# Routing with the first weights' splits behind the gathers and low parts on GpSimd; last sums, squares, statistics and output by quarters ahead of the general path

## Chip, core and metric

One Trainium2 chip, one core of it. The metric is device time in microseconds (us) of one execution; it is given as the median of several runs. Engines are called as in the profile: PE (TensorE; PEld is its weight load), DVE (VectorE), ACT (ScalarE), POOL (GpSimd), SP (SyncE, which issues most transfers). PE's clock has two levels, 1.2 and 2.4 GHz; the profile gives the granted clock as a share of the upper one.

## What is computed

A trunk of two pre-norm residual layers over 256 tokens of width 1024. Each has a mixer (a convolution branch and a bidirectional state-space branch); the first has a dense SwiGLU after it, the second eight SwiGLU experts of which each token takes two. A final RMSNorm gives the output. The change touches only the second layer's expert part and the final norm:

```python
def top2_moe(h, router_w, router_b, w_gate, w_up, w_down):
    t = h.reshape(bsz * seq_len, d)
    logits = (t @ router_w + router_b).astype(jnp.float32)
    top_val, top_idx = lax.top_k(logits, TOP_K)
    top_w = jax.nn.softmax(top_val, axis=-1)
    gates = jnp.sum(one_hot(top_idx, 8) * top_w[..., None], axis=1)
    for e in range(8):
        out = out + gates[:, e:e+1] * swiglu(t, w_gate[e], w_up[e], w_down[e])
...
x = x + top2_moe(rms_norm(x, g), ...)
return rms_norm(x, final_norm_g)
```

## The kernel before

Activations lie transposed: `x` is 8 tiles of 128 channels by 256 tokens. Precision comes from splitting a float32 operand into a rounded high part and a low part (`fp32r`), so a product of two split operands is three matmuls.

**Order.** Each engine runs its instructions in the order in which the Python code was executed: `ordered()` chains PE, DVE and ACT, and for the experts SP too. An instruction that waits therefore holds up everything behind it on its engine.

**Routing** (`route`, a generator, L1189). The router's logits come from `route_feed`, with the mean square of each token. `rms_of` turns it into `rs` (`rms_s`, 12 small DVE instructions). Then DVE makes `lg` (logits), the two largest, and `asg` (who goes where); PE counts tokens per expert (`rank`); DVE turns the ranks into one-hot matrices `oh`. Meanwhile `turn` transposes the normed activations on PE (tile `misc` in PSUM, two buffers), ACT rounds them to `hth`, and DVE takes the rest as `htl`. After the first one-hot, `alone` gathers expert 0's tokens: eight groups of four matmuls `misc<-oh,hth` and `misc<-oh,htl`, each copied out by ACT. The rest of the generator orders the experts by load (`ei`), gives each its ranks (`srank`) and gates (`gr`), and writes 14 further one-hots. `gate_rs(0)` multiplies `gr` by `oh`, and DVE copies the result (`gs`).

**Weights** (`moe_stream`). SP loads 1 MB at a time into 8 buffers `raw`. For the five fullest experts (j < NL) each half of a load is split by ACT into `wh` and by DVE into `wl` (L93, L75 through `split`); a pair is called a unit here. There are four buffers each of `wh` and `wl`. `get()` first fills a queue up to three units ahead, then takes one. `get.prime()` only fills. Before routing starts, `moe` calls `get.prime()`, so three units are split ahead of the routing.

**Experts** (`moe`). `first(v)` multiplies gate and up weights (four units, six matmuls each), `second(v)` the down weights (two units) into `py`. After an expert's last block, `back` scales `py` by the gate (ACT `yh`, DVE `yl`), `oht(j)` transposes the one-hot (PE, then a copy by ACT), and PE multiplies the two back into token order, in four quarters that `into` adds to `x`. The three emptiest experts do the same unsplit (`back_few`, `ys`).

**End.** `rest` is a general path for an expert with more than 128 tokens; it is skipped by a branch on `cnt` on every engine. Behind it `final` takes squares of `x` (ACT, `sq`), sums them on PE with 16 one-column products (32 passes in the trace), makes the scale (12 DVE instructions, two transposes, an ACT copy), scales `x` in eight pieces `o` and stores four quarters from SP.

Of the kernel before, what the change touches and what calls it, by code (L numbers as in the profile page):

```python
# [19 lines left out]
T = 256  # L20
# [8 lines left out]
NB = DFF // 256  # L29
# [29 lines left out]
class Body:  # L59
# [1129 lines left out]
    def route(self):  # L1189
        nc = self.nc  # L1190
        sp = self.rp
        hth = self.slot("hth", [128, 2, D], F32R)
        htl = self.slot("htl", [128, 2, D], F32R)
        self.hth, self.htl = hth, htl

        def turn(k4, b):

            ps = self.misc()
            for k in range(4):
                self.tr(ps[:, k * 128:(k + 1) * 128], self.xg[k4][:, k, b * 128:(b + 1) * 128])  # L1200
            s = slice(512 * k4, 512 * k4 + 512)
            nc.scalar.activation(hth[:, b, s], ps, AF.Copy)

            def low():
                self.sub(htl[:, b, s], ps, hth[:, b, s].bitcast(F32))
            return low

        pl = self.acc()
        for b in range(2):
            nc.tensor.transpose(pl[:, b * 8:b * 8 + 8], self.lt[:, b * 128:(b + 1) * 128], self.ident[0:8, 0:8])  # L1210
        lows = [turn(0, b) for b in range(2)]
        rs = self.rs

        gr = sp.tile([128, 2, NE, 2], F32, name="gr0")
# [32 lines left out]
        self.sub(d[:, :, 0], mx[:, :, 0], mx[:, :, 1])  # L1247
        self.sub(d[:, :, 1], mx[:, :, 1], mx[:, :, 0])
        nc.scalar.activation(d, d, AF.Tanh, scale=0.5)
        for f in lows:  # L1250
            f()
        lows = [turn(1, b) for b in range(2)]

        rank = sp.tile([128, 2, NE], F32, name="rank")
        self.stt(rank, ps[:, 0:16].rearrange("p (b e) -> p b e", b=2), 1.0, asg, ALU.add, ALU.mult)
# [2 lines left out]
        self.oh = oh  # L1258
        for b in range(2):
            nc.vector.tensor_scalar(oh[:, b, 0], self.iota, rank[:, b, 0:1], None, op0=ALU.is_equal)  # L1260
        for f in lows:
            f()
        yield
        nc.vector.tensor_scalar(d, d, 0.5, 0.5, op0=ALU.mult, op1=ALU.add)
        nc.vector.tensor_copy(gr[:, :, :, 1], two(rs))
# [66 lines left out]
    def moe_stream(self, items, ahead):  # L1332

        items, ready = deque(items), deque()
        first = [True]

        def prep():
            j, w, at, split = items.popleft()
            raw = self.raw8()
            src = self.a[w][(self.expert_of(j),) + at].rearrange("o p f -> p (o f)")  # L1340
            ins = self.nc.sync.dma_start(raw, src)
            if first[0]:
                self.behind(ins.ins, self.last_raw.ins)
                first[0] = False
            if split:
                for h in range(2):
                    yield self.split(raw[:, 1024 * h:1024 * h + 1024], 1024)
            else:
                yield raw

        now = [iter(())]

        def prime():
            while len(ready) <= ahead:
                u = next(now[0], None)
                if u is None:
                    if not items:
                        return
                    now[0] = prep()
                    u = next(now[0])  # L1360
                ready.append(u)

        def get():
            prime()
            return ready.popleft()
        get.prime = prime
        return get

    def moe(self):
# [18 lines left out]
                j, b = seq[t - 1]  # L1388
                items.append((j, "m_down", (b,), j < NL))
        get = self.moe_stream(items, 2)  # L1390
        get.prime()
        route = self.route()
        next(route)
        oh = self.oh
# [53 lines left out]
                tok[e + i] = [lambda k, h=h, i=i: tiles[h](k)[:, i] for h in range(2)]  # L1448

        def gather1():  # L1450
            x = [self.slot("x1", [128, 8, 2, 128], F32R) for _ in range(2)]
# [57 lines left out]
            self.sub(al, pv, ah.bitcast(F32))  # L1509
            return ah, al  # L1510

        py, pys = {}, {}
        extra = deque()

        def second(v, a):
            j, b = v
            last = b == NB - 1
            if j >= NL:
                if b == 0:
                    pys[j] = self.psx.tile([128, 512], F32, name="pys")  # L1520
                w = get()
                for k in range(2):
                    for h in range(2):
                        self.mm(pys[j][64 * h:64 * h + 64], a[:, 64 * k:64 * k + 64],
                                w[:, 1024 * k + 512 * h:1024 * k + 512 * h + 512], b == 0 and k == 0, last and k == 1)
                if last:
                    extra.append(back_few(j, pys.pop(j)))
                    next(extra[-1])
                return
            if b == 0:  # L1530
                py[j] = self.psx.tile([128, D], F32, name="py")
            ah, al = a
# [20 lines left out]
        def into(i, ps):  # L1553
            xq = self.x[:, 2 * i:2 * i + 2]
            self.add(xq, xq, ps.rearrange("p (f t) -> p f t", f=2))
            self.sums[i] += 1
            if self.sums[i] == NE:
                self.last_sum(i)

        def back(j, py):  # L1560
# [6 lines left out]
            o = oht(j, F32R)  # L1567
            yield
            for i in range(4):
                ps = self.misc()  # L1570
# [8 lines left out]
        def back_few(j, py):  # L1579
            y = self.ep.tile([128, 512], F32, name="ys")  # L1580
            nc.scalar.activation(y, py, AF.Copy, scale=gss[j][:, 0:1])
            o = oht(j, F32)
            yield
            for i in range(4):
                ps = self.misc()
# [17 lines left out]
                gate_rs(j)  # L1603
            yield

        self.sums = [0] * 4
        alone()
        for _ in route:
            pass
        gate_rs(0)  # L1610
        side = deque([small(), rates(range(NL, NE)), gather1(), rates(range(1, NL))])
        sl = None
# [23 lines left out]
                    side.popleft()  # L1636
        while extra:
            more()

    def rest(self):  # L1640

# [2 lines left out]
        with tc.If(n > self.cap):  # L1644
            hf = [t.bitcast(F32) for t in (self.hth, self.htl)]
            with tc.For_i(0, NE, 1) as e:
# [49 lines left out]
                for d in range(8):  # L1696
                    ps = self.misc()
                    self.mm(ps[:, :T], y[:, d * 128:(d + 1) * 128], oht, True, True)
                    self.add(self.x[:, d], self.x[:, d], ps[:, :T])

    def moe_consts(self):
        nc, cp = self.nc, self.cp
# [9 lines left out]

    def last_sum(self, i):

        pass

    def final(self):
        nc = self.nc
        rs, rb = self.rms_stat()
        g = self.col("gfin")  # L1720
        dst = self.out.rearrange("(k p) t -> p k t", p=128)
        o = self.slot("o", [128, 8, T])
        for k in range(8):
            self.stt(o[:, k], self.x[:, k], g[:, k:k + 1], rb, ALU.mult, ALU.mult)
            if k % 2:
                nc.sync.dma_start(dst[:, k - 1:k + 1], o[:, k - 1:k + 1])

    def specs(self):

# [66 lines left out]
    def run(self):  # L1796
        pool = self.pool
        with ExitStack() as ctx:
# [44 lines left out]
            with ExitStack() as c2:  # L1843
                self.sp = pool(c2, "slotf", 1)
                self.final()


_NAMES = ("xt", "par", "cdg", "bc", "bd", "w_in", "w_cproj", "w_glu", "w_sproj", "w_out", "f_gate", "f_up",
# [87 lines left out]
```

## Time and profile before

| | |
|---|---|
| runs | 1428.27 us median of 3 (1427.89 to 1429.31) |
| profiled execution | 1430.8 us, span 1429.0 us, mean granted clock 0.972 |
| busy | PE 1341.0 us (94%), PEld 1079.3 (76%), DVE 952.3 (67%), ACT 686.1 (48%), POOL 84.3 (6%) |
| routing, from the last products with `x` to the first expert product | 663.0 to 681.9 us |
| experts | 681.9 to 1409.0 us |
| final norm and output | 1409.0 to 1429.0 us |

The span runs from the first to the last instruction of one core. A busy PE is not PE at its peak. An idle stretch of an engine costs time only if the engine is the one the end waits for; in the expert stage that is PE, while in routing and in the final norm one engine after the other is waited for.

### The profile page before, as it was taken

The numbers are of one execution on the slowest core, as the hardware profiler recorded it, in microseconds if no ns is written. First come the engines' busy times: TensorE is split into PE (matmuls) and PEld (weight loads), VectorE is DVE, ScalarE is ACT, GpSimd is POOL, SyncE is SP. The second block draws the span as 40 slices with busy tenths as digits, with TensorE's granted clock in tenths as the row PEclk, the third lists the DMA queues.
The fourth block names the chain that finished last, engine by engine and source line by source line (L and its number), as shares of the span: only waits on it lengthen the run. The fifth ranks groups of instructions, "written<-read, shape, count | busy, mean of one in ns | idle before, by whom it ended". The sixth has DMA issues, their size and how long they took to land. (4 is left out here: it accounts for less than half of the span.)

```text
span 1429.0 us, 23540 instructions
## 1 busy us (share of the span) xinstructions
PE 1341.0 (94%) x9291; PEld 1079.3 (76%) x9291; DVE 952.3 (67%) x1413; ACT 686.1 (48%) x968; POOL 84.3 (6%) x148
## 2 busy tenths in 40 slices
PE   6989989999998969888999999999999999999995
PEld 5868879999998858886876666667676676666663
DVE  7696675788885465765775665667666666666663
ACT  3432344454444524443675555555555555555551
POOL 1052220000120040000000000000000000000000
PEclk9999999999999989998999999999999999999996
DMA  5284444566678394564689999998999999999970
GB/s 218 97 258 150 168 133 150 191 220 207 221 234 285 132 299 130 180 222 159 236 313 362 394 347 407 405 417 338 405 421 419 365 418 351 414 368 416 409 301 31
DMA packets 78307, 399.73 MB, mean 280 GB/s; under 512 B 13024, under 2 KB 15728, under 8 KB 44400
## 3 DMA queue, kind: packets, MB, share of 16 engines
q1 hardware_dynamic: 65504, 371.22, 68.0%
q0 software_dynamic: 8448, 26.31, 5.7%
q8 instruction: 75, 1.23, 0.4%
q10 hardware_dynamic: 4240, 0.64, 0.3%
q14 instruction: 40, 0.33, 0.1%
HBM read 386.51 MB, written 11.62 MB: 279 GB/s over the span
## 5 line engine op out<-in xcount | busy, mean ns | idle before, releaser
L75 DVE TENSOR_TENSOR wl<-raw,wh 128x1024 fp32r<-128x1024 f32 x460 | 549.5, 1222 | 220.5 <-ACT wh L93 220.2
L93 ACT ACTIVATE wh<-raw 128x1024 fp32r<-128x1024 f32 x460 | 470.5, 1054 | 77.1 <-issue 35.8
L116 PE MATMUL acc<-wh,x 128*128 128x512 f32 x880 | 293.9, 401 | 0.0
L116 PEld LDWEIGHTS acc<-wh,x 128*128 128x128 f32 x880 | 165.5, 188 | 44.9 <-ACT wh L93 8.9
L116 PE MATMUL acc<-wl,x 128*128 128x512 f32 x440 | 173.0, 393 | 0.0
L116 PE MATMUL acc<-hf,wh 128*128 128x256 f32 x704 | 128.4, 285 | 0.0
L116 PE MATMUL acc<-raw,xs 128*64 128x256 f32 x1056 | 127.9, 384 | 0.0
L116 PE MATMUL acc<-hh,wh 128*128 128x256 f32 x352 | 105.1, 298 | 7.0 <-ACT hh L636 3.1
L116 PE MATMUL acc<-xg,raw 128*128 128x256 f32 x448 | 103.2, 388 | 6.8 <-DMA raw<-in_w_in 6.8
L116 PEld LDWEIGHTS acc<-hf,wh 128*128 128x128 f32 x704 | 109.0, 190 | 0.2
L116 PEld LDWEIGHTS acc<-raw,xs 128*64 128x64 f32 x1056 | 71.2, 137 | 46.9 <-issue 17.5
L116 PE MATMUL acc<-hh,wl 128*128 128x256 f32 x352 | 103.0, 293 | 1.7 <-DVE wl L75 1.7
L116 PE MATMUL acc<-hl,wh 128*128 128x256 f32 x352 | 102.9, 292 | 0.0
L116 PE MATMUL acc<-hf,wl 128*128 128x256 f32 x352 | 99.9, 284 | 2.0 <-DVE wl L75 2.0
L116 PEld LDWEIGHTS acc<-xg,raw 128*128 128x128 f32 x448 | 85.8, 195 | 19.1 <-ACT xg L682 6.8
L116 PEld LDWEIGHTS acc<-wl,x 128*128 128x128 f32 x440 | 83.1, 189 | 18.0 <-DVE wl L75 1.7
L116 PE MATMUL py<-wh,mah 128*128 128x512 f32 x220 | 89.6, 407 | 0.0
L116 PE MATMUL py<-wh,mal 128*128 128x512 f32 x220 | 86.1, 391 | 0.0
L116 PE MATMUL py<-wl,mah 128*128 128x512 f32 x220 | 86.0, 391 | 0.0
L1508 ACT ACTIVATE mah<-misc 128x256 fp32r<-128x256 f32 x55 | 21.1, 384 | 128.6 <-PE misc L124 128.3
L116 PEld LDWEIGHTS acc<-hh,wh 128*128 128x128 f32 x352 | 70.7, 201 | 10.8 <-issue 4.0
L75 DVE TENSOR_TENSOR mal<-misc,mah 128x256 fp32r<-128x256 f32 x55 | 23.3, 423 | 74.9 <-ACT mah L1508 74.8
(290 smaller groups left out, 2002.6 us busy)
## 6 DMA issues: line engine op xcount, KB each, us to landing
raw<-in_m_gu SPq DMA_DIRECT2D x176, 1024.0 KB, 8.0
raw<-in_m_down SPq DMA_DIRECT2D x88, 1024.0 KB, 8.3
raw<-in_w_in SPq DMA_DIRECT2D x56, 512.0 KB, 4.1
raw<-in_f_gate SPq DMA_DIRECT2D x22, 512.0 KB, 3.5
raw<-in_f_up SPq DMA_DIRECT2D x22, 512.0 KB, 3.7
raw<-in_f_down SPq DMA_DIRECT2D x22, 512.0 KB, 3.5
raw<-in_w_out SPq DMA_DIRECT2D x16, 512.0 KB, 3.5
hs<-hc POOLq DMA_DIRECT2D x32, 142.0 KB, 5.4
```

The lines of the kernel that those rows point to most:

```text
L75: return self.nc.vector.tensor_tensor(out, a, b, op=op)
L93: self.nc.scalar.activation(h, raw, AF.Copy)
L116: return self.nc.tensor.matmul(out, l, r, start=start, stop=stop, **kw)
L1508: nc.scalar.activation(ah, pv, AF.Copy)
```

## The change

Five edits.

1. `moe` no longer calls `get.prime()` ahead of routing. Instead the loop that drains the routing generator calls `get.one()` at each of its steps, which splits one unit if fewer than three are ready. This loop stands behind `alone`.
2. All four `turn`s stand together ahead of the ranks. ACT copies `misc` a second time, to SBUF (`full`), and POOL subtracts `htl = full - hth`; DVE did this from PSUM.
3. `oht(j)` is made one block earlier, ahead of the products of block NB-2.
4. `last_sum`, called when a quarter of `x` has its last sum, takes that quarter's squares and the product of `x` with the final norm's weights (`o`, ACT). The quarter's products with `ones` are queued, and issued on PE behind the next quarter's add.
5. `finish` makes the scale and multiplies the four quarters of `o` by it straight from PSUM, and stores them from SP and ACT in turn. It stands ahead of the branch on `cnt`. The general path ends in its own `final`. For this the slots `x1` are taken first.

```diff
@@ route
+        self.x1 = [self.slot("x1", [128, 8, 2, 128], F32R) for _ in range(2)]
...
+            full = self.c2("full", [128, 512])
             nc.scalar.activation(hth[:, b, s], ps, AF.Copy)
-            def low():
-                self.sub(htl[:, b, s], ps, hth[:, b, s].bitcast(F32))
-            return low
+            nc.scalar.copy(full, ps)
+            nc.gpsimd.tensor_tensor(htl[:, b, s], full, hth[:, b, s].bitcast(F32), op=ALU.subtract)
...
-        lows = [turn(0, b) for b in range(2)]
+        for k4 in range(2):
+            for b in range(2):
+                turn(k4, b)
@@ moe_stream
+        def one():
+            n = len(ready)
+            if n <= ahead:
+                prime(n)
@@ moe
-        get.prime()
         route = self.route()
...
@@ second
+                if b == NB - 2:
+                    ohts[j] = oht(j, F32)
...
             if self.sums[i] == NE:
+                while self.queued:
+                    self.queued.pop(0)()
                 self.last_sum(i)
...
         alone()
         for _ in route:
-            pass
+            get.one()
...
         while extra:
             more()
+        self.finish()
@@ last_sum
+        sq = self.c2("sq", [128, 2, T])
+        nc.scalar.activation(sq, self.x[:, 2 * i:2 * i + 2], AF.Square)
+        for k in (2 * i, 2 * i + 1):
+            nc.scalar.activation(self.o[:, k], self.x[:, k], AF.Copy, scale=g[:, k:k + 1])
+        def products():
+            for d in range(2):
+                for b in range(2):
+                    self.mm(self.fin[:, b:b + 1], sq[:, d, b * 128:(b + 1) * 128], self.ones, ...)
+        self.queued.append(products)
@@ finish
+        rs = self.rms_of(self.fin[:, :2])
+        ps = self.acc()
+        for b in range(2):
+            self.tr(ps[:, b * 128:(b + 1) * 128], rs[:, b:b + 1].to_broadcast([128, 128]))
+        for i in range(4):
+            oq = self.o[:, 2 * i:2 * i + 2]
+            self.mul(oq, oq, ps[:, None, :T].to_broadcast([128, 2, T]))
+            (nc.sync, nc.scalar)[i % 2].dma_start(dst[:, 2 * i:2 * i + 2], oq)
```

On ACT, from the rounding of the gates' difference (`dd`) to the splits, before (`x_7275` and `x_7276` are expert 0's gathered high and low parts):

```order
L1249 ACTIVATE dd<-dd 128x4
L1202 ACTIVATE hth<-misc 128x512 x2
L1431 CAST x_7275<-misc 128x256
L1431 CAST x_7276<-misc 128x256
L1431 CAST x_7275<-misc 128x256
L1431 CAST x_7276<-misc 128x256
L1431 CAST x_7275<-misc 128x256
L1431 CAST x_7276<-misc 128x256
L1431 CAST x_7275<-misc 128x256
L1431 CAST x_7276<-misc 128x256
L93 ACTIVATE wh<-raw 128x1024 x4
```

The same place on ACT in the change (the gathered parts are `x_7269` and `x_7270`):

```order
L1205 COPY full<-misc 128x512
L1251 ACTIVATE dd<-dd 128x4
L1432 CAST x_7269<-misc 128x256
L1432 CAST x_7270<-misc 128x256
L1432 CAST x_7269<-misc 128x256
L1432 CAST x_7270<-misc 128x256
L1432 CAST x_7269<-misc 128x256
L1432 CAST x_7270<-misc 128x256
L1432 CAST x_7269<-misc 128x256
L1432 CAST x_7270<-misc 128x256
L93 ACTIVATE wh<-raw 128x1024 x7
```

The three `wh` that stood ahead of the first `hth` now stand behind the last of the eight copies.

On DVE, from the second rank sum to the one-hots, before:

```order
L1290 TENSOR_REDUCE srank<-t 128x8
L75 TENSOR_TENSOR t<-pm,gr 128x64
L1294 TENSOR_REDUCE gr<-t 128x8
L75 TENSOR_TENSOR t<-pm,gr 128x64
L1294 TENSOR_REDUCE gr<-t 128x8
L1295 COPY gr<-rms_s 128x16
L1301 TENSOR_SCALAR oh<-iota,srank 128x128 x14
```

In the change (here `t_7343` and `gr_7234` are single buffers of `t` and `gr`):

```order
L1287 TENSOR_REDUCE srank<-t_7343 128x8
L75 TENSOR_TENSOR wl<-raw,wh 128x1024
L75 TENSOR_TENSOR t_7343<-pm,gr_7234 128x64
L1291 TENSOR_REDUCE gr<-t_7343 128x8
L75 TENSOR_TENSOR t_7343<-pm,gr_7234 128x64
L1291 TENSOR_REDUCE gr<-t_7343 128x8
L1292 COPY gr<-rms_s 128x16
L75 TENSOR_TENSOR wl<-raw,wh 128x1024
L1298 TENSOR_SCALAR oh<-iota,srank 128x128 x14
```

A further `wl` stands between `ei` and `pm`, the first of the rank sums. The three `wl` stood ahead of `lg` before.

On PE, the end of the experts, before (`oht_13145` is the last small expert's transposed one-hot):

```order
L116 MATMUL misc<-oht_13118,yh 128x256
L116 MATMUL misc<-oht_13118,yl 128x256
L116 MATMUL misc<-oht_13145,ys 128x256 x8
L1643 TENSOR_LOAD cnt
L1644 COMPARE_AND_BRANCH
```

In the change (`oht_13072` is that one-hot, `acc` the sums of squares):

```order
L116 MATMUL misc<-oht_13072,ys 128x256 x4
L116 MATMUL acc<-ones,sq 128x1 x4
L116 MATMUL misc<-oht_13072,ys 128x256 x2
L116 MATMUL acc<-ones,sq 128x1 x4
L116 MATMUL misc<-oht_13072,ys 128x256 x2
L116 MATMUL acc<-ones,sq 128x1 x8
L124 MATMUL acc<-ident,rms_s 128x128 x2
L1651 TENSOR_LOAD cnt
L1652 COMPARE_AND_BRANCH
```

The sums of squares moved from behind the branch to between the last experts' products, and the two transposes of the scale with them.

## Rows read from the trace of the kernel before

**Rows 1.** Busy time, granted clock and transfers by stage (window, length, engines, PEclk, DMA share, GB/s).

```profile
665.40:675.40 10.00, 4.12 (x19) 3.72 (x19) 7.89 (x25) 2.23 (x5) 0.00 (x0) 0.51 0.32 119
681.90:1394.40 712.50, 704.63 (x3668) 498.50 (x3669) 460.90 (x518) 396.75 (x539) 0.57 (x1) 1.00 0.94 376
```

**Rows 2.** Timeline of routing (start, length in us, instruction, idle before and its releaser).

```profile
665.36 3.50 DVE L75 TENSOR_TENSOR wl<-raw,wh 128x1024 fp32r<-128x1024 f32 x3
668.77 0.17 DVE L75 TENSOR_TENSOR lg<-acc,rms_s 128x16 f32<-128x16 f32 x1
673.06 0.17 DVE L87 SCALAR_TENSOR_TENSOR rank<-acc,asg 128x16 f32<-128x16 f32 x1 [1.06 <-PE acc L116]
674.64 0.69 DVE L75 TENSOR_TENSOR htl<-misc,hth 128x512 fp32r<-128x512 f32 x1 [0.67 <-ACT hth L1202]
675.38 0.93 PEld L116 LDWEIGHTS misc<-oh,hth 128*128 128x128 f32 x4 [0.96 <-DVE htl L75]
677.76 0.22 DVE L75 TENSOR_TENSOR pm<-iota,sf 128x64 f32<-128x64 f32 x1
680.03 2.83 DVE L1301 TENSOR_SCALAR oh<-iota,srank 128x128 fp32r<-128x128 f32 x14
681.41 0.59 PE L116 MATMUL misc<-gr,oh 128*128 128x2 f32 x4
681.87 0.49 PE L116 MATMUL acc<-wh,x 128*128 128x512 f32 x1
681.88 1.06 ACT L93 ACTIVATE wh<-raw 128x1024 fp32r<-128x1024 f32 x1
683.86 1.20 DVE L75 TENSOR_TENSOR wl<-raw,wh 128x1024 fp32r<-128x1024 f32 x1
687.50 0.51 PE L116 MATMUL misc<-oh,hth 128*128 128x384 f32 x2
```

**Rows 3.** Two us behind the last sum (columns as in Rows 1).

```profile
1409.00:1411.00 2.00, 0.00 (x0) 0.00 (x0) 0.00 (x0) 1.67 (x3) 0.00 (x0) 0.68 0.00 0
```

**Rows 4.** PE's waits from 683 to 1405 us (us in total, times, longest).

```profile
PE misc L116 <- ACT oht L1550: 6.5, 7, 1.2
PE misc L116 <- DVE yl L87: 2.7, 4, 0.7
```

**Rows 5.** All engines' waits from 800 to 1390 us, the weight loads of second products.

```profile
PEld py L116 <- ACT wh L93: 11.1, 29, 0.4
```

**Rows 6.** The GpSimd group of the largest mean, before 640 us.

```profile
L347 POOL COPY tabo<-pw 64x256 f32<-64x256 f32 x6 | 6.9, 1156 | 0.3
```

**Rows 7.** Timeline of the last expert and the final norm.

```profile
1397.07 0.39 PE L116 MATMUL misc<-oht,yl 128*128 128x256 f32 x1 [0.67 <-DVE yl L87]
...
1404.36 3.90 PE L116 MATMUL misc<-oht,ys 64*128 64x256 f32 x16
1408.30 0.69 DVE L75 TENSOR_TENSOR x<-x,misc 128x512 f32<-128x512 f32 x1 [0.18 <-PE misc L116]
1409.22 1.67 ACT L219 ACTIVATE sq<-x 128x512 f32<-128x512 f32 x3 [5.65 <-DVEq L1644]
1411.69 6.95 PE L116 MATMUL misc<-ones,sq 128*128 128x1 f32 x32 [3.43 <-PEq L1644]
1418.68 0.16 DVE L225 TENSOR_SCALAR rms_v<-misc 128x2 f32<-128x2 f32 x1 [9.69 <-PE misc L116]
1421.06 0.69 PE L124 MATMUL misc<-ident,rms_s 128*128 128x128 f32 x2 [2.42 <-DVE rms_s L87]
1422.19 3.25 DVE L87 SCALAR_TENSOR_TENSOR o<-x,par,rstdb 128x256 f32<-128x256 f32 x8 [1.19 <-ACT rstdb L145]
1423.10 2.75 SPq L1726 DMA_DIRECT2D out_t<-o  x4
```

**Rows 8.** SP's waits from 683 to 1400 us, at the branch.

```profile
SPq L1644 <- SPq L1644: 7.4, 2, 5.2
```

**Rows 9.** Issues of the output (KB each, median us to landing).

```profile
out_t<-o SPq DMA_DIRECT2D x4, 256.0 KB, 2.2
```

More of the change, by code (lines that the diff above doesn't have):

```diff
@@ L1249, in route @@
         nc.scalar.activation(d, d, AF.Tanh, scale=0.5)
-        for f in lows:
-            f()
-        lows = [turn(1, b) for b in range(2)]
         rank = sp.tile([128, 2, NE], F32, name="rank")
@@ L1260, in route @@
             nc.vector.tensor_scalar(oh[:, b, 0], self.iota, rank[:, b, 0:1], None, op0=ALU.is_equal)
-        for f in lows:
-            f()
         yield
@@ L1351, in moe_stream, with prime @@
         now = [iter(())]
-        def prime():
-            while len(ready) <= ahead:
+        def prime(n=ahead):
+            while len(ready) <= n:
                 u = next(now[0], None)
@@ L1365, in get @@
             return ready.popleft()
-        get.prime = prime
+        def one():
+            n = len(ready)
+            if n <= ahead:
+                prime(n)
+        get.prime, get.one = prime, one
         return get
@@ L1450, in gather1 @@
         def gather1():
-            x = [self.slot("x1", [128, 8, 2, 128], F32R) for _ in range(2)]
+            x = self.x1
             both([lambda k, h=h: x[h][:, k] for h in range(2)], 1)
@@ L1510, in turned @@
             return ah, al
-        py, pys = {}, {}
+        py, pys, ohts = {}, {}, {}
         extra = deque()
@@ L1531, in second @@
                 py[j] = self.psx.tile([128, D], F32, name="py")
+            if b == NB - 2:
+                ohts[j] = oht(j, F32R)
             ah, al = a
@@ L1566, in back @@
             self.stt(yl, py, gs[:, 0:1], yh.bitcast(F32), ALU.mult, ALU.subtract)
-            o = oht(j, F32R)
+            o = ohts.pop(j)
             yield
@@ L1581, in back_few @@
             nc.scalar.activation(y, py, AF.Copy, scale=gss[j][:, 0:1])
-            o = oht(j, F32)
+            o = ohts.pop(j)
             yield
@@ L1604, in rates @@
             yield
-        self.sums = [0] * 4
+        self.sums, self.queued = [0] * 4, []
         alone()
         for _ in route:
-            pass
+            get.one()
         gate_rs(0)
@@ L1699, in rest @@
                     self.add(self.x[:, d], self.x[:, d], ps[:, :T])
+            self.final()
     def moe_consts(self):
@@ L1713, in last_sum, with finish @@
     def last_sum(self, i):
-        pass
+        nc = self.nc
+        g = self.col("gfin")
+        if i == 0:
+            self.o = self.slot("o", [128, 8, T])
+            self.fin = self.acc()
+        sq = self.c2("sq", [128, 2, T])
[5 more added lines that the diff above has]
+                for b in range(2):
+                    self.mm(self.fin[:, b:b + 1], sq[:, d, b * 128:(b + 1) * 128], self.ones,
+                            i + d + b == 0, i == 3 and d == 1, skip_group_check=True)
+        self.queued.append(products)
+    def finish(self):
+        nc = self.nc
+        for f in self.queued:
+            f()
+        rs = self.rms_of(self.fin[:, :2])
+        ps = self.acc()
+        for b in range(2):
+            self.tr(ps[:, b * 128:(b + 1) * 128], rs[:, b:b + 1].to_broadcast([128, 128]))
+        dst = self.out.rearrange("(k p) t -> p k t", p=128)
+        for i in range(4):
+            oq = self.o[:, 2 * i:2 * i + 2]
+            self.mul(oq, oq, ps[:, None, :T].to_broadcast([128, 2, T]))
+            (nc.sync, nc.scalar)[i % 2].dma_start(dst[:, 2 * i:2 * i + 2], oq)
     def final(self):
@@ L1721, in final @@
         dst = self.out.rearrange("(k p) t -> p k t", p=128)
[L1722 to L1726, printed above, removed]
+        for i in range(4):
+            o = self.gp.tile([128, 2, T], F32, name="g_o")
+            for d in range(2):
+                k = 2 * i + d
+                self.stt(o[:, d], self.x[:, k], g[:, k:k + 1], rb, ALU.mult, ALU.mult)
+            nc.sync.dma_start(dst[:, 2 * i:2 * i + 2], o)
     def specs(self):
@@ L1842, in run @@
             keep.close()
-            with ExitStack() as c2:
-                self.sp = pool(c2, "slotf", 1)
-                self.final()
 _NAMES = ("xt", "par", "cdg", "bc", "bd", "w_in", "w_cproj", "w_glu", "w_sproj", "w_out", "f_gate", "f_up",
```

## Prediction

> **What bounds the kernel now.** I read the busy time by stage first, then the timelines of the two stages the change touches, then PE's waits between them. From 682 to 1394 us PE is busy 704.63 of 712.50 us at the full clock [rows 1]: whatever makes the first expert product later or earlier moves the end by as much, and a later load doesn't, while buffers are full. In the 10 us of routing before, PE is busy 4.12 and DVE 7.89, with the clock at 0.51, which is the lower level for nearly all of it [rows 1]. The reader is to see a chain there: `wl` (665.36, three of them, 3.50 us) holds up `lg` (668.77), which waits for nothing else; then counting (`rank` 673.06), the one-hot, and a wait of PE for `htl` until the first gather at 675.38; the gates' product at 681.41; the first expert product at 681.87 [rows 2]. At the end there is a second chain, without overlap: last add 1408.30, squares, 6.95 us of one-column products behind 3.43 us in which PE waits for its own sequencer at the branch, statistics, scaling from 1422.19, stores from 1423.10 [rows 7].
>
> **Edits 1 and 2, routing.** *Removed:* three `wl` from ahead of `lg`, so `lg` comes at 665.4, 3.3 us earlier, and `rank` at 669.75. Before, the one-hot then waited for the third `htl` until 675.33 (674.64 + 0.69); it was itself ready one `rank` and two one-hot writes after 673.06, by about 673.96. Now ACT evacuates all four turns from about 663.8, eight copies of some 0.55 us (the square of the same size, three in 1.67 [rows 7]), done by 668.2. The first gather comes at 670.65: 4.7 us earlier.
>
> *Moved:* the three splits stand behind the eight copies of the gathered tokens on ACT, and on DVE between the steps that order the experts. I take the eight gathers to last as before, 675.38 to 681.41, 6.03 us [rows 2]. PE then reaches the gates' product at 676.7 and ACT the first `wh` at 677.3. From here I walk DVE's new order, with `wh` at 1.06, `wl` at 1.20, and the two halves of the ordering together 2.27 (677.76 to 680.03) [rows 2]:
>
> - `wh` done 678.35; DVE, which finished `ei` long before, has waited for it; first `wl` done 679.55.
> - rank sums 1.28 → 680.85; second `wl` → 682.05; gates 1.0 → 683.05. Only now can PE do the gates' product, which it has waited for since 676.7. It takes 0.46 (681.41 to 681.87), so the first expert product starts at 683.5, not 681.87.
> - third `wl` → 684.3; 14 one-hots 2.83 → 687.1; count and `gs` as before 1.0 (682.86 to 683.86) → 688.1; fourth `wl` → 689.3.
> - PE needs 5.63 us for the four units (681.87 to 687.50), 1.41 each. Three end at 687.7; PE waits for the fourth `wl` until 689.3, and its other five of six products end at 690.5. Before: 687.50.
>
> So 4.7 us gained on the routing chain become **3.0 us lost** on the first block: the splits were in the way of the logits, but they overlapped with PE's transposes, and now they stand behind the gathers and in the way of the gates. What is behind them there is the whole expert stage. The bounds: if the lower clock (0.51 [rows 1]) did not come at all, counting would take half of its 2.3 us and the gathers would follow their copies; the same walk ends 0.2 us late. If the lower clock held through all gathers it ends 3.5 late.
>
> *Low parts on POOL.* No row shows a subtraction there. A copy of 64x256 with one input takes 1156 ns [rows 6], and the DVE instruction replaced takes 0.69 [rows 2]. For 512 elements that is 0.69 from below; from above twice the copy for twice the elements and twice that for two inputs, 4.6 us. Up to 2.5 us each, four in a row (from 664.9) end before the last pair is read, at the sixth gather, 670.65 + 5 × 0.8; I take 1.5, nearer to the DVE row because the work is contiguous: nothing. The Trainium skill ("GPSIMD Engine Reference", section 3, Performance versus the Vector engine) advises VectorE for elementwise work and has a two-input add of 2048 elements at 4497 ns against 2293. By it one subtraction is an estimated 1.1 us, slower than what it replaces and hidden all the same, so that the sum stays; no run here shows it yet.
>
> *Loads.* The load that waits for the first `raw` leaves some 13 us later. Eight buffers of two units are full then, over 20 us of PE's work at 1.41 a unit: nothing.
>
> **Edit 3, earlier one-hots.** PE's wait for `oht` is 6.5 us in 7 places [rows 4], which looks like the gain. But behind it stands the wait for `yl` (2.7 in 4), and `yl` ends when `yh` and it are done, not when `oht` is; in the last expert it comes at 1397.07 [rows 7], and no edit moves it. For the full experts nothing comes forward; the two transposes, hidden in that wait before, cost about 0.23 us each time elsewhere, unless they fall into one of the 29 waits of 0.4 us for `wh` ahead of the second products [rows 5]. The small ones gain what they pay. I take **0.2 us lost** (0 to 1.0).
>
> **Edits 4 and 5, the end.** With the transposes of `oht` gone the last additions of the first two quarters come about 0.25 us earlier. Four quarters of products take PE 3.90 us before, 0.97 each [rows 7]; a quarter's sums of squares are a fourth of 6.95, 1.74 at the lower clock [rows 3, 7], half of that at the upper. New chain: add of quarter 0 at 1405.3 to 1406.0; its square to 1406.7; its sums, 0.9, between quarters 1 and 2; add 2 at 1408.9; sums of quarter 1; then the clock falls as at 1409.7 before (0.68 over 1409 to 1411 [rows 3]), so quarter 3's products and add end at 1412.1; square 0.63; sums 1.74 and their drain → 1414.7; statistics 2.38 (1418.68 to 1421.06) → 1417.1; transposes 0.73 → 1417.8. Multiplication from PSUM replaces the copy and the weighted scaling. Four of these, 0.6 to 0.7 us apart, are no slower than the eight `o` (3.25). Scaling thus starts 4.4 us before 1422.19. With the clock up throughout it is 6.0, with all of it down 4.1.
>
> What the branch cost does not vanish. Before, PE paid 3.43 us in the middle, and the other engines could branch while they were idle. Now all of them branch behind their last product or store, SP too, and the program ends when they are through. The landing of the last store, 2.2 us [rows 9], covers part of it. SP's waits at its branch were 7.4 us, the longer one 5.2 [rows 8], which can include the landing of its last weights. From below: the branch hides behind the landing, nothing shows. From above: 5.2 less 2.2 leaves 3.0. I take PE's 3.43 as SP's price, nearest in kind, which leaves 1.2. **Net 3.2 us gained** (4.4 less 1.2; from 4.1 − 3.0 = 1.1 to 6.0). The Trainium skill ("Runtime: NRT & Kernel Launch", section Instruction fetch mechanics) says that a taken branch out of the fetched window stalls until its target is fetched. PE's wait for its sequencer agrees, 3.43 us; whether SP's branch does so the trace can't tell.
>
> **Sum.** Against the profiled execution: +3.0 + 0.2 − 3.2 = 0.0: the span stays at 1429.0 and the execution at 1430.8. The profiled execution is 2.5 us above the median of the runs shown; on the median the forecast is **1428.3 us**, no change.
>
> **Rivals.** What a measurement of this kernel can tell from no change is about 0.2%, 2.9 us.
>
> - *The clock stays up.* PE's pauses in routing become shorter, so the lower level may come later or go sooner, and the sums of squares keep PE busy at the end. Then +0.2, 0.0 and, with the branch hidden too, −6.0: 1422.5 us; 1425.3 with the branch at 3.0. Against it: transposes and one-column products are all PE does from 664 to 670, as before, when the clock fell.
> - *POOL is the bound.* The four subtractions follow each other, so each us above 2.6 costs four: with 4.6 the walk ends 11 us late, and with the other terms at −3.0 that is 1436 us. It decides from 3.3 us on, where four times 0.7 on top of routing's 3.0 bring the sum to +2.9. Only the doubled copy speaks for it.
> - *The end is not gained.* SP's branch at 5.2 us and the lower clock leave 1.1, and with routing at its bound of 3.5 that is +2.6, 1430.9 us.
> - *Edit 3 gives back the 6.5 us* of its row: 1422 us. The wait for `yl` behind it speaks against it; I give it next to nothing.
>
> **How the numbers follow.** My forecast and its neighbours within 2.9 us: 0.72. The clock staying up, in whole or far enough, and edit 3: 0.17. POOL 0.05, the end lost with routing at its bound and a little of edit 3's upper bound 0.06: 0.11 slower. The range takes in the third rival, and of the first the part with the branch visible: 1424.9 to 1431.0 us.
>
> **What would show it.** Right: first gather near 670.7; PE waiting for DVE's `gr` ahead of the gates' product from about 677; first `wl` behind the last copy; first expert product near 683.5 and small gathers near 690.5; no wait for `oht` but longer ones for `yh`; scaling some 6.4 us behind the last add's start against 13.9 before; SP silent for some us behind its last store. Wrong: a first expert product before 681 (the walk fails), gathers waiting for POOL, or an end 7 us or less behind the start of scaling (the branch hidden; it was 6.8 before, and the forecast is 8.0).

## The result: slower, 1440.5 us against 1428.8

The changed kernel takes 1440.5 us (1434.3 to 1441.8) where the kernel before took 1428.8 beside it: 1.0075 times, 95% interval 1.0048 to 1.0102. The forecast was no change, 1428.3 us, range to 1431.0.

The profiled execution is the fastest of these, 1434.3 us with a span of 1432.1. Its front, the same code as before, happens to be 5 us shorter: routing's mean square comes at 657.96, and in the kernel before at 663.11. So the two are compared from that row on. It is one row of the timeline of before that stands in none of the groups:

```profile
663.11 0.16 DVE L225 TENSOR_SCALAR rms_v<-misc 128x2 f32<-128x2 f32 x1 [3.20 <-PE misc L116]
```

The timeline of the changed kernel, routing and then the end, to be held against [rows 2] and [rows 7]:

```profile
657.96 0.16 DVE L225 TENSOR_SCALAR rms_v<-misc 128x2 f32<-128x2 f32 x1 [3.20 <-PE misc L116]
...
660.04 4.94 POOL L1206 TENSOR_TENSOR htl<-full,hth 128x512 fp32r<-128x512 f32 x4 [91.78 <-ACT full L1205]
...
660.13 1.20 DVE L87 SCALAR_TENSOR_TENSOR rms_s<-rs_t,rms_s 128x2 f32<-128x2 f32 x1
...
661.43 0.17 DVE L75 TENSOR_TENSOR lg<-acc,rms_s 128x16 f32<-128x16 f32 x1
661.64 0.93 DVE L75 TENSOR_TENSOR lg<-lg,par 128x16 f32<-128x16 f32 x1
...
663.82 1.27 DVE L75 TENSOR_TENSOR s<-iota,xf 128x16 f32<-128x16 f32 x2
...
668.62 1.19 PE L116 MATMUL misc<-oh,hth 128*128 128x256 f32 x4 [0.96 <-DVE oh L1259]
...
675.63 3.89 ACT L93 ACTIVATE wh<-raw 128x1024 fp32r<-128x1024 f32 x4
676.72 1.23 DVE L75 TENSOR_TENSOR wl<-raw,wh 128x1024 fp32r<-128x1024 f32 x1 [6.37 <-ACT wh L93]
...
681.36 0.99 PE L116 MATMUL misc<-gr,oh 128*128 128x2 f32 x4 [6.04 <-DVE gr L1292]
...
682.78 0.63 PE L116 MATMUL acc<-wl,x 128*128 128x512 f32 x1
...
690.42 0.51 PE L116 MATMUL misc<-oh,hth 128*128 128x384 f32 x2
...
1407.36 1.96 PE L116 MATMUL misc<-oht,ys 64*128 64x256 f32 x8 [0.40 <-DVE x L75]
1409.96 1.05 PE L116 MATMUL acc<-ones,sq 128*128 128x1 f32 x8 [0.64 <-ACT sq L1730]
1410.94 1.59 PE L116 MATMUL misc<-oht,ys 64*128 64x256 f32 x4
1412.46 1.87 PE L116 MATMUL acc<-ones,sq 128*128 128x1 f32 x8
1414.25 2.07 PE L116 MATMUL misc<-oht,ys 64*128 64x256 f32 x4
1416.36 0.69 DVE L75 TENSOR_TENSOR x<-x,misc 128x512 f32<-128x512 f32 x1 [3.11 <-PE misc L116]
1423.04 2.48 DVE L75 TENSOR_TENSOR o<-o,acc 128x512 f32<-128x512 f32 x4 [0.85 <-PE acc L124]
```

| stretch, us | before | forecast | after |
|---|---|---|---|
| mean square to first gather | 12.27 | 7.54 | 10.66 |
| first gather to gates' product | 6.03 | 12.40 | 12.74 |
| gates' product to small gathers | 6.09 | 7.45 | 9.06 |
| small gathers to the last expert's `ys` products | 716.86 | 717.1 | 716.94 |
| `ys` products to scaling | 17.83 | 13.4 | 15.68 |
| scaling to the end | 6.81 | 8.0 | 9.06 |

PE waits for the gates for 6.04 us (681.36), where before it went from the gathers to the gates' product without one; behind that wait the first products run at the lower clock (0.63 us, not 0.39). And while POOL subtracts, small instructions of DVE are long: `rms_s` 1.20 in place of 0.16, the second `lg` 0.93 in place of some 0.17, two `s` 1.27 in place of 0.26, together 2.8 us more. The first `lg`, between them, reads PSUM (`acc`) and keeps its 0.17. From the mean square to the end it is 8.2 us more, and routing has nearly all of it (8.1).

Held against the terms of the forecast, this execution has +8.1 us for routing and the first block where +3.0 was forecast, +0.1 for edit 3 where it was +0.2, and +0.1 for the end where it was −3.2. The medians lie 11.7 us apart; the other 3.5 do not show in this execution, the fastest of its four.

PE's waits between 683 and 1405 us, to be held against [rows 4] (9.2 us in all there, 10.1 here):

```profile
PE misc L116 <- ACT yh L1572: 4.8, 4, 1.2
PE misc L116 <- DVE yl L87: 3.7, 4, 0.9
PE misc L116 <- ACT ys L1588: 1.6, 2, 0.8
```

### The profile page after: what moved, and what is told of

The parts are those of the page before. It is cut to its first block, busy times and chain, and to the rows that moved or that the text cites. A ratio compares the mean times of both kernels' runs of the same rounds, so it can differ in the third digit from the quotient of the medians.

```text
span 1432.1 us, 23557 instructions
## 1 busy us (share of the span) xinstructions
PE 1347.4 (94%) x9291; PEld 1087.2 (76%) x9291; DVE 951.5 (66%) x1405; ACT 690.6 (48%) x979; POOL 89.3 (6%) x152
## 4 chain that ended last, share of the span: by engine, by line
PE 50%; DVE 1%; ACT 1%; issue 0%; DVEq 0%; ACTq 0%
PE acc L116 31%; PE py L116 11%; PE pys L116 4%; PE misc L116 3%; PE misc L124 2%; DVE yl L87 0%; ACT yh L1572 0%; DVE x L75 0%; DVE wl L75 0%; DVE o L75 0%; ACT ys L1588 0%; DVE t L75 0%; PE acc L124 0%; ACT sq L1730 0%; ACT x L1410 0%
## 5 line engine op out<-in xcount | busy, mean ns | idle before, releaser
L116 PE MATMUL acc<-xg,raw 128*128 128x256 f32 x448 | 107.1, 398 | 6.6 <-ACT xg L682 6.6
```

Of the source, the lines that this page charges most:

```text
L116: return self.nc.tensor.matmul(out, l, r, start=start, stop=stop, **kw)
```

## The experiments

The theory after the first profile: two parts of routing cost the time, the splits in the way of the gates (edit 1) and POOL's subtractions beside DVE (edit 2). The rivals: one of them alone, edit 3, the end, or the front. "Routing" below is the mean square to the small gathers, worked out from each profile's timeline; ratios are against the kernel before on the same chip, with 95% intervals; "one" is a single execution.

| kernel | us, median | ratio | routing, us |
|---|---|---|---|
| before (six series); `before_look` | 1426.1 to 1428.8; 1424.5 (one) | 1 | 24.4; 24.5 |
| `after_again` | 1440.1 | 1.0088 (1.0062 to 1.0115) | 30.8 |
| `after_look` | 1440.7 (one) | | 32.7 |
| `after_third` | 1436.6 | 1.0069 (1.0044 to 1.0094) | 32.4 |
| `splits_ahead` (without 1) | 1434.9 | 1.0042 (1.0028 to 1.0056) | 26.8 |
| `splits_ep`; `splits_look` (both without 1) | 1432.2; 1430.4 (one) | 1.0049 (1.0031 to 1.0066) | 26.8; 26.7 |
| `low_on_dve` (without 2) | 1433.8 | 1.0037 (1.0022 to 1.0052) | 30.0 |
| `end_onehot_only` (3 to 5) | 1427.3 | 0.9995 (0.9979 to 1.0010) | 24.2 |
| `end_only` (4 and 5) | 1429.8 | 1.0012 (0.9996 to 1.0028) | 24.4 |
| `onehot_only` (3) | 1428.3 | 1.0003 (0.9987 to 1.0018) | 24.5 |
| `pool_beside` | 1431.1 | 1.0025 (1.0010 to 1.0040) | 25.9 |
| `end_lazy` | 1427.1 | 0.9994 (0.9980 to 1.0007) | 22.3 |
| `after_late_onehot` (without 3) | 1438.1 | 1.0068 (1.0050 to 1.0087) | 33.1 |
| `after_filled` | 1436.3 | 1.0057 (1.0038 to 1.0076) | 32.4 |
| `lazy_filled`; again | 1425.9; 1425.2 | 0.9983 (0.9967 to 0.9999); 0.9982 (0.9967 to 0.9997) | 22.3; 22.3 |
| `sums_last` | 1423.6 | 0.9970 (0.9953 to 0.9988) | 22.3 |

**The changed kernel again, and each half of routing undone.** `after_again` has no edit.

> The changed kernel itself, once more, as the control for the three beside it. Its runs so far were 1434.3 to 1441.8 us against 1428.8, and the profiled one was the fastest, with a front (the same code) some 5 us shorter than that of the profile before. If the front merely differs from execution to execution, the median stays at 1438 to 1442 us and the profile shows either front; from the routing's mean square to the small gathers it stays near 32.4 us (24.4 before).

`splits_ahead` undoes edit 1:

```diff
+        get.prime()
         route = self.route()
...
-            get.one()
+            pass
```

> Edit 1 undone: the three splits ahead of routing again, the other four edits kept. My theory, that the splits behind the gathers delay the gates and the first block by 4 to 6 us: 6 us below the changed kernel, with the small gathers some 27 us behind the mean square (24.4 before, 32.4 in the change). Rival, that POOL's subtractions are what slows routing: within 2 us of the changed kernel, the small gathers still more than 30 us behind.

`low_on_dve` undoes edit 2 (turns and `low` as before), and `end_onehot_only` both:

```diff
...
-            nc.gpsimd.tensor_tensor(htl[:, b, s], full, hth[:, b, s].bitcast(F32), op=ALU.subtract)
...
+            def low():
+                self.sub(htl[:, b, s], ps, hth[:, b, s].bitcast(F32))
...
```

> Edit 2 undone: two turns after the other and the low parts on DVE from PSUM, with no work on POOL; the other four edits kept. My theory gives POOL's subtractions 2.5 to 3 us (the small DVE instructions beside them took 0.9 to 1.3 us in place of 0.16 to 0.26): 2 to 3 us below the changed kernel, with those instructions back at 0.16 to 0.26. The rival gives them all of the routing's loss: 8 us below.

> Edits 1 and 2 undone, so that routing is that of before; the earlier one-hots and the end by quarters kept. My theory: all of the loss is in routing, and the end's 1.6 to 3 us remain: 1425.5 to 1427.5 us. Rival, that the loss is behind routing (in the expert stage, or in buffers that lie elsewhere): 1432 us or more.

Without edit 1 the time falls by 5.3 us, without edit 2 by 6.4, without both by 12.8, to the kernel before. So both count, neither alone, and edits 3 to 5 together cost nothing that can be told. In the profiles they add up too: routing is 2.4 us longer with edit 2 alone, 5.6 with edit 1 alone, 8.1 with both. For edit 2 the 2 to 3 us that were expected are in the profiles, and not in the medians (6.4). The timeline of `low_on_dve`:

```profile
661.32 0.16 DVE L225 TENSOR_SCALAR rms_v<-misc 128x2 f32<-128x2 f32 x1 [3.20 <-PE misc L116]
...
663.97 0.17 DVE L75 TENSOR_TENSOR lg<-lg,par 128x16 f32<-128x16 f32 x1
...
670.38 1.22 PE L116 MATMUL misc<-oh,hth 128*128 128x256 f32 x4 [0.56 <-DVE htl L75]
...
678.01 1.23 DVE L75 TENSOR_TENSOR wl<-raw,wh 128x1024 fp32r<-128x1024 f32 x1 [5.16 <-ACT wh L93]
...
682.66 0.98 PE L116 MATMUL misc<-gr,oh 128*128 128x2 f32 x4 [6.05 <-DVE gr L1296]
```

Without POOL the second `lg` is back at 0.17 us and the first gather comes 9.06 us behind the mean square, 3.2 earlier than before. But PE's wait for the gates is the same 6.05. And `splits_ahead`, where the splits run beside POOL:

```profile
661.22 5.64 DVE L75 TENSOR_TENSOR wl<-raw,wh 128x1024 fp32r<-128x1024 f32 x3
662.28 6.92 POOL L1206 TENSOR_TENSOR htl<-full,hth 128x512 fp32r<-128x512 f32 x4 [92.79 <-ACT full L1205]
...
673.05 1.19 PE L116 MATMUL misc<-oh,hth 128*128 128x256 f32 x4 [0.96 <-DVE oh L1259]
...
679.71 0.61 PE L116 MATMUL misc<-gr,oh 128*128 128x2 f32 x4
```

Three `wl` take 5.64 us against 3.50 [rows 2], POOL's four 6.92 against 4.94; the gates' product waits for nothing.

**Single parts.** `end_only` undoes edit 3 too, `onehot_only` is edit 3 on the kernel before. `pool_beside` adds work for POOL that nobody waits for:

```diff
             nc.scalar.activation(hth[:, b, s], ps, AF.Copy)
+            h = hth[:, b, s].bitcast(F32)
+            nc.gpsimd.tensor_tensor(self.c2("full", [128, 512]), h, h, op=ALU.subtract)
```

> The kernel before with four subtractions on POOL added to routing, one behind each rounding of a turn, of a high part from itself into a buffer that nobody reads; no other engine waits for them. If POOL's work slows the small DVE instructions beside it, those take 0.9 to 1.3 us in place of 0.16 to 0.26, and routing is 2 to 3 us longer: 1430.5 to 1431.5 us. Rival: they were slow for another reason (the copies of ACT, the order), so they stay at 0.16 to 0.26 and the time at 1428.4 us.

```profile
659.92 5.18 DVE L75 TENSOR_TENSOR wl<-raw,wh 128x1024 fp32r<-128x1024 f32 x3
660.52 3.50 POOL L1204 TENSOR_TENSOR full<-hth 128x512 f32<-128x512 f32 x2 [90.16 <-ACT hth L1202]
...
670.88 0.69 DVE L75 TENSOR_TENSOR htl<-misc,hth 128x512 fp32r<-128x512 f32 x1 [0.67 <-ACT hth L1202]
670.93 2.04 POOL L1204 TENSOR_TENSOR full<-hth 128x512 f32<-128x512 f32 x2 [6.91 <-ACT hth L1202]
```

The cost is shown, 2.7 us by the medians and 1.5 in routing's profile, though not where I looked: the small instructions kept their length, since in this order POOL meets the three `wl`, 5.18 us in place of 3.50. Beside DVE's `htl`, which reads PSUM, POOL takes 1.02 us each and `htl` its 0.69; beside `wl`, which reads two tiles of SBUF, POOL takes 1.75. The Trainium skill ("SBUF — State Buffer", section SBUF: two separate sides) says that a DVE instruction with two SBUF inputs and a GpSimd instruction that reads SBUF exclude each other for the whole of an instruction. These rows agree: the three `wl` are 1.68 us longer, and two subtractions of POOL take 2.04 where they meet no such instruction. Two instructions with one input were longer as well, by less (`xf` 0.36 us in place of 0.17 in the changed kernel, `dd` 0.64 in place of 0.16 here); no run separates why.

> Edits 4 and 5 alone (the end by quarters, ahead of the branch); routing and one-hots as before. Theory now: edit 3 costs 2 to 3.7 us in the expert stage, because without the transposes in PE's pause after a second product the granted clock falls there (0.83 over 10 us in one or two such places of each profile with edit 3, 1.00 in all three of the profile before). Then the clock stays at 1.00 at those places and this is 2 to 3 us below the kernel with edits 3 to 5 (1427.3): 1424 to 1425.5 us. Rival: edit 3 costs the 0.2 us that I predicted, and the end is worth only 1 us: 1427 us.

> Edit 3 alone, the earlier one-hots. By the theory of the falling clock 2 to 3.7 us slower than before, 1430.5 to 1432 us, with a granted clock of 0.83 over 10 us at one or more of the three waits for yh and yl after full experts. Rival: 0.2 us, 1428.6 us, and the clock at 1.00 there.

The falling-clock theory of edit 3 fell. `end_only` is no faster than with edit 3, `onehot_only` no slower than before, and the clock falls behind full experts with or without the earlier one-hots.

`end_lazy` keeps edits 4 and 5 and moves only the DVE half of the three splits; the roundings stay ahead of routing on ACT:

```diff
         self.nc.scalar.activation(h, raw, AF.Copy)
-        self.sub(lo, raw, h.bitcast(F32))
+        if self.lazy is None:
+            self.sub(lo, raw, h.bitcast(F32))
+        else:
+            self.lazy.append(lambda: self.sub(lo, raw, h.bitcast(F32)))
```

> Edits 4 and 5, and in place of edit 1 only the DVE half of the three splits is moved off the logits' chain: the three roundings stay ahead of routing on ACT, and the subtractions stand behind the first low parts, behind the second ones, and behind the gates. If a split costs nothing where DVE waits anyway, logits come 2.4 us behind the mean square in place of 5.7, the first gather 9 to 10 in place of 12.3, the small gathers 21.5 to 23 in place of 24.2: 1 to 2.5 us below edits 4 and 5 alone. Rival: what is gained on the logits is lost behind the gathers, as in the change: no difference to edits 4 and 5 alone.

Routing was 22.3 us, 2.1 less than before, as expected; the median is 2.7 us below `end_only`. The first gather comes at 9.06 behind the mean square as in `low_on_dve`, but the gates' product at 15.1, not 21.3.

**Where a typical execution is.** `before_look`, `after_look` and `splits_look` are further profiles, the last of them without edit 1; `splits_ep`, without edit 1 too, puts `full` into two idle buffers:

```diff
-            full = self.c2("full", [128, 512])
+            full = bufs[k4][:, 512 * b:512 * b + 512].bitcast(F32)
```

> The kernel before, once more, for a second profile of it. If the falls of the clock behind full experts come by chance, whatever the kernel, this profile can show 0.83 over 10 us at one of the three places, and the time from the small gathers to the last product is then 717 to 719 us in place of 715.3; the front (to routing's mean square) lies anywhere from 655 to 665 us, routing at 24.2 us.

> The changed kernel, for a third profile of it. Both profiles so far have a front of 658 and 662.5 us and 30.5 to 32.2 us from the mean square to the small gathers; a typical time of 1440 us needs 664 us of front, or a routing some 4 us longer still. Theory A: routing stays at 30 to 32 us, and the front is 664 us or more when the time is 1440 us. Theory B: routing itself varies, up to 36 us.

> The kernel with edit 1 undone, for a second profile of it. Its profiled execution was the fastest of its 12 (1430.4 us; median 1434.9). Theory A: routing again 26.6 us and a longer front. Theory B: a longer routing, up to 30 us, with POOL's subtractions and the DVE instructions beside them longer than before.

> The kernel with edit 1 undone (1434.9 us), with the copies `full` in two buffers that exist already (those of yh and yl, unused until the first expert ends) in place of three new ones that lie below the front's. By the profiles edit 2 makes routing 2.6 us longer, by the medians the kernel is 6.7 us slower. Theory A: the rest is the front, where buffers moved: 1431 us here, the routing as before (small gathers 26.6 us behind the mean square). Theory B: the place of the buffers doesn't matter, and the medians and single profiles differ by chance or by something else in routing: 1434 to 1436 us.

Both theories for `after_look` missed, and `splits_look` met another fast execution and so decided nothing. `after_look` (1440.7 us) has the front of the fastest execution (mean square at 658.30) and routing's 32.7 us; its 6 us more lie in the expert stage, where the clock falls four times behind pauses of PE, and in the fastest execution once; three falls more, at 1.7 us each (worked out below), are 5.1 of the 6. Windows of `after_look`, and then the same places of the changed kernel's first profile (columns as in [rows 1]):

```profile
815.00:825.00 10.00, 7.87 (x32) 6.13 (x31) 5.81 (x6) 3.29 (x4) 0.00 (x0) 0.83 0.81 336
965.00:970.00 5.00, 5.00 (x17) 3.91 (x17) 2.88 (x4) 2.15 (x3) 0.00 (x0) 0.66 0.96 400
1115.00:1125.00 10.00, 7.86 (x45) 4.55 (x45) 5.07 (x6) 4.36 (x6) 0.00 (x0) 0.83 0.64 238
1265.00:1270.00 5.00, 4.23 (x23) 2.90 (x23) 3.23 (x4) 0.34 (x1) 0.00 (x0) 0.66 0.50 208
```

```profile
815.00:825.00 10.00, 8.02 (x31) 6.63 (x32) 5.19 (x6) 3.17 (x4) 0.00 (x0) 0.83 0.76 319
965.00:970.00 5.00, 5.00 (x24) 4.04 (x24) 4.08 (x5) 3.23 (x4) 0.00 (x0) 1.00 0.99 388
1110.00:1120.00 10.00, 7.86 (x51) 5.31 (x51) 5.39 (x7) 3.75 (x5) 0.00 (x0) 1.00 0.87 333
1260.00:1270.00 10.00, 8.57 (x56) 5.93 (x57) 7.57 (x9) 5.92 (x8) 0.00 (x0) 1.00 0.79 314
```

A share of 0.83 over 10 us, or 0.66 over 5, is 1.7 us of clock lost. The pause that brings it, from the timeline of `after_look`, is the end of an expert, with products of 0.39 us ahead and 0.63 behind:

```profile
815.08 0.39 PE L116 MATMUL py<-wh,mal 128*128 128x512 f32 x1
816.67 0.39 PE L116 MATMUL misc<-oht,yh 128*128 128x256 f32 x1 [1.20 <-ACT yh L1572]
817.98 0.39 PE L116 MATMUL misc<-oht,yl 128*128 128x256 f32 x1 [0.93 <-DVE yl L87]
...
819.84 0.63 PE L116 MATMUL acc<-wl,x 128*128 128x512 f32 x1
```

In all four profiles of the changed kernel PE waits 1.2 and 0.9 us there; whether the clock falls differs from execution to execution, in kernels with and without the change (`before_look` has none, with its mean square at 658.4; `pool_beside` has one, `end_lazy` three). The place of `full` makes no difference that can be told, and `splits_look` repeats `splits_ahead` within 0.2 us.

**Are these falls part of the cost?** `after_third` is the changed kernel again, `after_late_onehot` undoes edit 3 in it, `after_filled` gives PE work that nobody reads in its waits for `yh`, `yl` and `ys`, and `lazy_filled` is `end_lazy` with the same work:

```diff
+        def fill(ps, j, n):
+            for b in range(n):
+                self.tr(ps[:, b % 4 * 128:b % 4 * 128 + 128], ohf[:, 0, j])
...
+                    if not i + d:
+                        fill(f, j, 5)
                     self.mm(ps[:, d * T:(d + 1) * T], yh[:, s], o, True, False)
+                    if not i + d:
+                        fill(f, j, 3)
```

> The changed kernel, as the control for the two beside it, and for a fourth profile. Its three profiles had 1, 1 and 4 stretches in the expert stage in which the granted clock fell behind a pause of PE, about 1.7 us each, at 1434.3, 1438.4 and 1440.7 us. If its median near 1440 us comes with several such falls, the profile of an execution near 1440 us shows three or four, unless its front is 662 us or more.

> The changed kernel with idle PE filled where it waits for yh, yl and ys: 5, 3 and 3 transposes of a one-hot into a buffer that nobody reads, at each expert's end (about 1.0 and 0.6 us, within the waits of 1.2, 0.9 and 0.8). If the pauses bring the clock down, it stays at 1.00 from the small gathers to the last big expert's end, and the time is 3 to 6 us below the changed kernel. Rival, that the falls have no part in the changed kernel's 1440 us: no lower time, or 0.5 to 1 us above for the transposes.

> The changed kernel with edit 3 undone: the one-hots are transposed in the pause at the expert's end again. If edit 3 matters because its longer unbroken pauses bring more falls of the clock, 2 to 4 us below the changed kernel with fewer falls; if it is worth what it was alone (1428.3 against 1428.4), within 1 us of the changed kernel.

> The best kernel so far (edits 4 and 5, and the DVE halves of the three splits in DVE's waits; 1427.1 us, three falls of the clock in its profile) with the same transposes in PE's waits. If each fall costs 1.7 us and the transposes prevent them, 1422 to 1425 us, with the clock at 1.00 from the small gathers to 1390 us; otherwise 1427 to 1428 us.

The fill does what it should: the profiles with it show no fall in the expert stage. The window of `end_lazy` around the end of expert 0, and of `lazy_filled`:

```profile
803.40:813.40 10.00, 8.08 (x33) 6.43 (x32) 6.17 (x8) 3.81 (x6) 0.00 (x0) 0.83 0.92 382
```

```profile
800.00:830.00 30.00, 28.65 (x171) 20.03 (x171) 16.65 (x21) 14.57 (x22) 0.00 (x0) 1.00 0.91 358
```

`after_filled` spreads less (1435.6 to 1439.4 us, against 1432.8 to 1444.3), but its median is that of `after_third`. So the falls can account for part of the spread, not for the loss: what remains without them is still 1.0057 times the kernel before, 8.1 us, as much as the profiles show in routing. `lazy_filled`, at 1425.9 and 1425.2 us, is 1 to 2 us below `end_lazy`, less than the three falls in that one profile would give. `after_late_onehot` is not faster: edit 3 is worth nothing here either.

**The end.** `sums_last` is `lazy_filled` with the one-column sums of three quarters moved behind all of the last expert's products; `lazy_filled_2` is its control:

```diff
-                while self.queued:
+                while i == 3 and self.queued:
```

> The best kernel so far once more (1425.9 us, ratio 0.9983 with an interval of 0.9967 to 0.9999), as the control for the one beside it and to see whether it stays below the kernel before: 1424 to 1427 us, no fall of the clock in the expert stage, 12.2 us from the last small expert's products to the mean square.

> The same with one edit: the one-column sums of the first three quarters stand behind all four quarters of the last small expert's products on PE, in place of between them. In the changed kernel those products and their adds took 9.0 us with the sums between (3.9 before), since PE waits there for squares and adds at the lower clock. If that is why scaling came only 2 to 3 us earlier where I predicted 4.4, the last add comes 3.9 to 4.5 us behind the first product here, the mean square 10.5 to 11.5 us in place of 12.2, and the time is 1 us below its control (within what can be told). Rival: the sums cost the same wherever they stand, and the mean square stays at 12 us.

The timeline of `sums_last`, and of its control:

```profile
1394.04 3.90 PE L121 MATMUL misc<-oht,ys 64*128 64x256 f32 x16
...
1397.87 6.14 PE L121 MATMUL acc<-ones,sq 128*128 128x1 f32 x32
1397.98 0.69 DVE L75 TENSOR_TENSOR x<-x,misc 128x512 f32<-128x512 f32 x1 [0.18 <-PE misc L121]
...
1404.05 0.16 DVE L230 TENSOR_SCALAR rms_v<-acc 128x2 f32<-128x2 f32 x1 [5.38 <-PE acc L121]
```

```profile
1398.32 1.56 PE L121 MATMUL misc<-oht,ys 64*128 64x256 f32 x6
...
1406.87 0.69 DVE L75 TENSOR_TENSOR x<-x,misc 128x512 f32<-128x512 f32 x1 [3.10 <-PE misc L121]
...
1410.37 0.16 DVE L230 TENSOR_SCALAR rms_v<-acc 128x2 f32<-128x2 f32 x1 [2.81 <-PE acc L121]
```

The last add comes 3.94 us behind the first product in place of 8.55, the mean square 10.0 in place of 12.05. By its median this kernel is the fastest of all, below both given ones; its 1.6 us to its control are within what the two intervals allow.

PE's stretch in which the changed kernel makes its last products (columns as in [rows 1]), and the waits of SP's own queue behind the last stores, in the changed kernel and in the one before:

```profile
1411.00:1417.00 6.00, 6.00 (x21) 4.44 (x20) 1.32 (x2) 2.44 (x6) 0.00 (x0) 0.54 0.00 0
```

```profile
SPq L1652 <- SPq L1652: 3.8, 1, 3.8
```

```profile
SPq L1932 <- DMA out_t<-o: 1.5, 1, 1.5
```

L1652 is the branch on `cnt`. In the changed kernel SP comes to it behind its last store, waits 3.8 us for its own sequencer, and then for no landing; before, it had branched by 1400 us [rows 8] and waited 1.5 us for the last store to land. All 16 profiles with edits 4 and 5 have the first wait (3.7 to 4.4 us) and not the second, the four without have the second.

## Why the prediction was wrong

- **Low parts on POOL: the step that failed in its mechanism.** I called them hidden at up to 2.5 us each and looked only for who waits for POOL. They are short (1.2 us) and nobody waits, as predicted; but while they read SBUF, DVE's instructions with two SBUF inputs wait. In the changed kernel 3.1 us of the 4.7 that I expected to gain ahead of the first gather are lost (7.54 forecast, 10.66 measured), and the longer rows of DVE (`rms_s`, `lg`, `s`) hold 2.8 of them. `pool_beside` shows the mechanism by itself, `low_on_dve` its absence. By medians edit 2 costs 6.4 to 7.5 us, by the profiles 2.4; the three profiled executions without edit 1 that keep edit 2 all took 1430 us, and what the others (to 1438 us) have more was not seen: open.
- **The walk of the moved splits held.** First gather to gates' product: 12.40 forecast, 12.74 measured; `low_on_dve` confirms it without POOL. By medians edit 1 costs 5.3 to 6.4 us.
- **The first block was mis-sized**, 7.45 forecast, 9.06 measured: I had PE at 1.41 us a unit, but behind its wait of 6 us the clock was at the lower level (0.63 us a product; granted 0.50 from 681.4 to 687.4 us, where the kernel before had 1.00). I had the clock's fall in the gathers only. With POOL's 3.1 and 0.3 of the walk these 1.6 make routing's +8.1 where I had +3.0.
- **The end was not gained.** Scaling came 2.15 us earlier (17.83 to 15.68), not 4.4, and the end 2.25 later behind it, not 1.2: nothing is left of the 3.2. The first miss is between the last expert's first product and the last add: 9.00 us, where my steps make it about 7.3 (1404.1 to 1411.4) and it was 3.94 before. PE waited for squares and adds for only 1.0 us of it (0.64 and 0.40); the sums of two quarters took 2.9, and the clock, which I had at the lower level for the last quarter alone, was there from 1411.5 us on (0.54 over 1411 to 1417), so that the second of these sums took 1.87 us in place of 0.9. With the sums behind the products, in `sums_last`, scaling comes 13.2 us behind the `ys` products. The second miss is the price of SP's branch: 3.8 us, not 3.43, and of the landing only 1.5 us could cover it, not 2.2, since SP had waited no longer than that for it. 3.8 less 1.5 is 2.3; the stores are issued 1.4 us sooner behind the start of scaling, and SP's further instructions behind the branch take about as much more.
- **Edit 3** was right: 0.2 forecast, `onehot_only` +0.4 by its ratio (interval −1.9 to +2.6), the wait for `oht` gone and those for `yh`, `yl` and `ys` in its place.
- **The rivals.** POOL's was the right engine with the wrong mechanism: I let it decide by making PE wait. The front and the clock's falls in the expert stage vary by several us in either kernel, which no term of mine held.

## What to carry to other kernels

Work moved to an idle GpSimd can be paid for by VectorE where both read SBUF: look at which small VectorE instructions with two SBUF inputs lie beside it, and whether these are a chain. Work moved off a chain must land in a wait of its engine: the three splits cost 5.6 us behind the gathers, and their subtractions alone, put into VectorE's waits with the roundings left ahead, gained 2.1. Where sums are taken by parts, a part's sum ahead of the next part's products delays these by its own length and by what it waits for. A branch that was hidden in the middle shows when it is moved behind the last store.

## What the runs showed of the hardware

Not expected: a pause of PE of 1.2 and 0.9 us at an expert's end, the same in every profile of the changed kernel, is followed by the lower clock in some places and not in others; each fall costs 1.7 us, and with 8 short transposes in the waits (3 at a small expert's end) none was seen in four profiles. A branch behind the last store held SP's queue for 3.7 to 4.4 us. And one subtraction of 128x512 on GpSimd took 1.02 us beside VectorE reading PSUM and 1.75 beside VectorE reading two SBUF tiles, which itself went from 1.17 to 1.73 us each (3.50 and 5.18 for three).
